# Splitting the output rows' weight pieces ahead of time, with a third place for them and loads from ACT's DMA queue

## The chip, the cores and the metric

The kernel runs on one core of a Trainium2 chip. The metric is the device time of one execution in microseconds (us), lower is better. The engines are named as in the profile: PE is TensorE's matmul, PEld its weight load, DVE is VectorE, ACT is ScalarE, POOL is GpSimd, SP is SyncE, which here only issues DMAs (SPq).

## What is computed

One layer of a streaming encoder over 2048 prompt tokens and 32 sample tokens, width 1024, all in float32. The reference, cut to what matters:

```python
h = layer_norm(x, ln_in_g, ln_in_b)
z = h @ w_in                                   # one projection for both mixers and the gates
y_a = gated_delta_net(conv4(z[qkv]), ...)      # 8 heads, blocks of 64 frames
y_b = z[B] * conv3(z[C] * z[u]) * silu(z[zb])  # short gated convolution
gates = sigmoid(z[gate])
merged = gates[:1024] * (y_a @ w_proj_a) + gates[1024:] * (y_b @ w_proj_b)
h1 = layer_norm(ALPHA * h + merged @ w_out, ln1_g, ln1_b)
ple = sigmoid(h1 @ w_ple_gate) * (p @ w_ple)
h2 = layer_norm(ALPHA * h1 + ple, ln2_g, ln2_b)
```

## The kernel before

**Precision.** Every matmul is made of three: an operand x is split into a high part `hi` (x cast to float32r) and a low part `lo = x - hi`, and the product is hi·hi + hi·lo + lo·hi. A weight piece of 128 x 1024 is split where it is first used (`load_w`): SP loads the raw piece into `wr`, ACT casts it into `wh` (L248), DVE or POOL subtracts into `wl` (L249), and SP stores both halves in DRAM (L251) for the next use, which loads the two halves (L243). `wr`, `wh` and `wl` have two places each, in the pool `wp`.

**Order of the work.** The tokens go in two halves (1024 prompt tokens and the 32 of the sample, then 1024). Each half has three parts:

1. *Projections.* A list of jobs, one for each block of 128 output columns. A job loads its weight piece, and PE makes groups of 24 matmuls of 352 (first half) or 512 columns into one of three accumulators `acc`; ACT or DVE takes the result out. `run` loads the next job's piece while a job runs. The delta rule's steps are interleaved by `fill.pump()`. The last eight jobs are gate jobs (`gate_a_job`): a sigmoid by ACT into a tile `ga`, which SP stores in DRAM.
2. *Merge* (`merge`): 24 jobs: five gate jobs for the other gate (`gb_`), eight for `w_proj_b` (`wb`), three gate jobs (`late`), eight for `w_proj_a` (`wa`), which load their gate back into `gt` (two places). `yh`, `yl` and `m` are tiles of 33,792 bytes a partition. ACT and DVE split the merged `m` into `xh`, `xl` (L970, L972).
3. *Output rows.* Here tokens are the stationary operand and weights move. `out_rows` (with `w_out`, `wo`) and then `ple_rows` (with `w_ple_gate`, `wg`) go over groups of four blocks of 128 tokens (in the first group of the first half also the sample), for each over two column halves `ch` of 512, and in each through four weight pieces `q` (`rows`). A piece serves 12 matmuls of 512 columns for each of its two k (14 with the sample's block), so 24 or 28 matmuls. When a column half is done, ACT and DVE add the residual and take statistics; when a group is done, DVE applies the LayerNorm, and PE transposes the rows (L223) into two places `pp`, from which ACT casts (L226) and DVE subtracts (L227) the next stationary operand. `pw` holds rows of p @ w_ple, which POOL multiplies with the sigmoid (L1088). `lnx` are the rows themselves. In the second half `hold` brings four pieces of `wg` into `xh`, `xl` ahead.

In the first half's rows the eight pieces of `wo` and the eight of `wg` are used for the first time, so they are split there, the subtraction by POOL. All later uses load the stored halves. All DMAs are issued by SP, in one queue.

**What sets the order.** A scheduler of the framework orders each engine's instructions at build time by priority and a model of time; on the chip each engine takes its list in order, and a tile's place is waited for by semaphore. Pools opened after others are closed lie on the same memory; their tiles wait for the tiles that lay there.

Of the kernel before, what the change touches and what calls it, by code (L numbers as in the profile page):

```python
# [20 lines left out]
NS = 32  # L21
HP = 1024
# [71 lines left out]
def hybrid_kernel(ctx: ExitStack, tc: tile.TileContext, I, O):  # L94
    nc = tc.nc
    ve, ac, po, pe = nc.vector, nc.scalar, nc.gpsimd, nc.tensor
# [3 lines left out]
    wp = ctx.enter_context(tc.tile_pool(name="wp", bufs=2))  # L100
# [59 lines left out]
    xh = cp.tile([128, KT, HP + 2 * NS], F32R, name="xh")  # L160
# [65 lines left out]
                ac.copy(out=oh, in_=p[:, :, :n])  # L226
                ve.tensor_tensor(out=lo[:, 4 * b:4 * b + 4, l0:l0 + n], in0=p[:, :, :n], in1=oh.bitcast(F32), op=ALU.subtract)  # L227

    def load_w(name, at, low, into=None):


        src, kept = I[name], split_d[name]
        for i in at:
            src, kept = src[i], kept[i]

        def cut(x):
            return x.rearrange("p (a b) -> p a b", a=2) if into else x

        parts = into or [wp.tile([128, 1024], F32R, tag=x, name=x) for x in ("wh", "wl")]
        hi, lo = parts  # L240
        if (name, at) in stored:
            for i, t in enumerate(parts):
                nc.sync.dma_start(out=t.bitcast(F32), in_=cut(kept[i]))  # L243
            return parts
        stored.add((name, at))
        raw = cut(wp.tile([128, HP + NS], F32, tag="wr", name="wr")[:, :1024])
        nc.sync.dma_start(out=raw, in_=cut(src))
        ac.copy(out=hi, in_=raw)  # L248
        low.tensor_tensor(out=lo, in0=raw, in1=hi.bitcast(F32), op=ALU.subtract)  # L249
# [643 lines left out]
    def gate_a_job(hf, c, gp):  # L893

        t = []

        def open():
            t.append(gp.tile([128, 1064], F32, tag=("ct", "cu")[c % 2], name="ga", bufs=1))

        def evac(a, g0, n):  # L900
            ac.activation(out=t[0][:, g0:g0 + n], in_=a[:, :n], func=AF.Sigmoid)

        def close():
            nc.sync.dma_start(out=ga_d[c, :, 0:hf.nt], in_=t[0][:, :hf.nt])

        return Job(("wz", BGA + c), hf.groups, evac, close, open)


    def merge(hf, mp):
        yh = mp.tile([128, KT, HP + NS], F32R, tag="yh", name="yh", bufs=1)  # L910
        m = mp.tile([128, KT, HP + NS], F32, tag="m", name="m", bufs=1)
        yl = mp.tile([128, KT, HP + NS], F32R, tag="yl", name="yl", bufs=1)

        def load_y(br, ks):
            for k in ks:
                raw = wp.tile([128, HP + NS], F32, tag="wr", name="yr")[:, :hf.nt]
                nc.sync.dma_start(out=raw, in_=y_d[br][k, :, 0:hf.nt])
                ac.copy(out=yh[:, k, :hf.nt], in_=raw)
                ve.tensor_tensor(out=yl[:, k, :hf.nt], in0=raw, in1=yh[:, k, :hf.nt].bitcast(F32), op=ALU.subtract)  # L919

        def loads_y(br, jobs):
# [12 lines left out]

        def evac_b(c, a, s):
            ve.tensor_tensor(out=m[:, c, s], in0=a[:, :s.stop - s.start], in1=m[:, c, s], op=ALU.mult)

        def evac_a(c, a, s):
            ve.tensor_tensor(out=gts[c][:, s], in0=a[:, :s.stop - s.start], in1=gts[c][:, s], op=ALU.mult)
            ve.tensor_tensor(out=m[:, c, s], in0=m[:, c, s], in1=gts[c][:, s], op=ALU.add)  # L940

        gts = {}

        def load_gate(c):
            gts[c] = mp.tile([128, HP + NS], F32, tag="gt", name="gt", bufs=2)
# [12 lines left out]
        gb_ = [gate(c, BGB, lambda c: m[:, c, :]) for c in range(5)]  # L958
        late = [late_gate(c) for c in range(5, KT)]
        wb = [branch(c, "wb", evac_b if c < 5 else plain) for c in range(KT)]  # L960
        wa = [branch(c, "wa", evac_a) for c in range(KT)]
        loads_y("b", gb_[:4])
        loads_y("a", wb[7:] + late)
        for c in range(KT):
            wa[c].open = lambda c=c: load_gate(c)
        run(gb_ + wb + late + wa)
        for g in hf.ogroups:
            for k in range(KT):
                for s in ([slice(g[0][0], g[0][0] + 512)] + ([slice(HP, HP + NS)] if len(g) > 4 else [])):
                    ac.copy(out=xh[:, k, s], in_=m[:, k, s])  # L970
                    low = xl[:, k, s] if s.start < HP else xh[:, k, HP + NS:]
                    ve.tensor_tensor(out=low, in0=m[:, k, s], in1=xh[:, k, s].bitcast(F32), op=ALU.subtract)  # L972


    def hold(q):

        load_w("wg", (1, q), po, [t[:, 2 * q:2 * q + 2, 512:HP] for t in (xh, xl)])

    def rows(src, npiece, kh, kl, cols, done, after=None, last=1):

# [12 lines left out]

        halves = [slice(0, 512), slice(512, 1024)]
        for q in range(npiece - last):
            w = load_w(*src(q), po)
            for kk in range(2):
                for a, (t0, n) in zip(accs, cols):  # L1000
                    step(a, t0, n, 2 * q + kk, *w, halves[kk])
            if after:
                after(q)
        ws = [load_w(*src(q), po) for q in range(npiece - last, npiece)]
        for a, (t0, n) in zip(accs, cols):
            for i, w in enumerate(ws):
                for kk in range(2):
# [27 lines left out]
        ve.tensor_tensor(out=t[:n], in0=t[:n], in1=a[:n], op=ALU.add)  # L1035
        return t[:n]

    def out_rows(hf, h1, lp, op, g1, b1):
        for gi, g in enumerate(hf.ogroups):
            xs, sts = [], []  # L1040
            for t0, n in g:
# [4 lines left out]
            for ch in range(2):  # L1046
                def done(a, n, i):
                    x = xs[i][:n, 512 * ch:512 * ch + 512]
                    ve.scalar_tensor_tensor(out=x, in0=x, scalar=ALPHA, in1=fold(a, n, op), op0=ALU.mult, op1=ALU.add)
                    ln_stats(sts[i], xs[i], n, ch)  # L1050

                rows(lambda q: ("wo", (ch, q)), 4, xh, xl, g, done)
            for i, (t0, n) in enumerate(g):
                ln_apply(xs[i:i + 1], n, sts[i:i + 1], g1, b1)
                nc.sync.dma_start(out=h1_d[hf.row0 + t0:hf.row0 + t0 + n, :], in_=xs[i][:n])
                fill.add(spaced(transpose_split(xs[i], n, *(h1[gi] if n > NS else h1[gi][:1] * 2), 128 * i, 128 * i + (NS if n == NS else 0)), 7 if i else 14))

    def ple_rows(hf, gi, h1, lp, op, g2, b2, end=False, hold=None, late=False):
        g = hf.ogroups[gi]
        xs, ws, sts = [], [], []  # L1060
        cols = [(128 * i, n) for i, (t0, n) in enumerate(g)]
# [14 lines left out]
        for ch in range(2):  # L1076
            pw = []
            by_tile = end and ch == 1
            for t0, n in g:
                w = op.tile([128, 512], F32, tag="pw", name="pw", bufs=4)  # L1080
                nc.sync.dma_start(out=w[:n], in_=pw_d[hf.row0 + t0:hf.row0 + t0 + n, 512 * ch:512 * ch + 512])
                pw.append(w)

# [12 lines left out]
            if by_tile:  # L1096
                rows_by_tile([(xh[:, k, 512:HP], xl[:, k, 512:HP]) for k in range(KT)], h1[gi][0], h1[gi][1], cols, done)
            else:
                rows(lambda q: ("wg", (ch, q)), 4, h1[gi][0], h1[gi][1], cols, done, (lambda q: q % 2 and hold(2 * ch + q // 2)) if hold else None, last=2 if late and ch else 1)
        if not (end or late):  # L1100
            for i in range(len(g)):
                finish(i)
# [14 lines left out]
    def ep():  # L1117
        return eps[-1]
# [17 lines left out]
    for hf in HALVES:  # L1136
        with pool(f"gp{hf.idx}") as gp:
# [28 lines left out]
            jobs += bj + [gate_a_job(hf, c, gp) for c in range(KT)]  # L1166
            fill.rate = [0.275, 0.56] if hf.sample else [0.41, 0.82]
            run(jobs, 3, *((True, lambda: deque(reload, 0)) if hf.idx else ()))
            fill.drain()
        early.close()  # L1170
        with pool(f"mp{hf.idx}") as mp:
# [3 lines left out]
        with pool(f"hp{hf.idx}") as op, pool(f"lp{hf.idx + 1}", 6) as lp, pool(f"gbp{hf.idx}") as gbp:  # L1175
# [2 lines left out]
            hs = [(h1h, h1l), (xh, xl)]  # L1178
            g1, b1, g2, b2 = gb(gbp, "ln_out", 4)
            fill.rate = [1.0, 1.0]  # L1180
            out_rows(hf, hs, lp, op, g1, b1)
            if hf.idx == 0:
                fill.add(reload_h(h1, lp, h1.blocks[4:8]))
            ple_rows(hf, 0, hs, lp, op, g2, b2, hold=hold if hf.idx else None)
            fill.drain()
            ple_rows(hf, 1, hs, lp, op, g2, b2, hf.idx == 1, late=hf.idx == 0)
            if hf.idx == 0:
                reload = reload_h(h1, lp, h1.blocks[0:4])
    for i, nm in enumerate("ps"):
# [84 lines left out]
```

## Time and profile before

| | |
|---|---|
| median of 3 runs | 3222.32 us (3219.36 to 3226.43) |
| the profiled execution's own time | 3223.0 us |
| its span, first to last instruction | 3221.3 us |
| mean granted clock of TensorE | 0.977 |
| PE busy | 3065.1 us, 95% of the span |
| DVE, ACT, POOL busy | 1911.1, 887.2, 225.4 us (59%, 28%, 7%) |
| DMA | 477.07 MB, mean 148 GB/s |
| bytes on the queue that SP issues to | 473.78 MB |

The span is what the views of the trace divide up; the time of the profiled execution is 1.7 us longer. PE is the bound of the kernel as a whole, but the share of its busy time is a mean over parts with different limits: the gate jobs of the first half run from about 1085 to 1183 us, its merge to 1462, its output rows to 1709; the second half's rows run from 2999 to 3205.

### The profile page before, as it was taken

The numbers are of one execution on the slowest core, as the hardware profiler recorded it, in microseconds if no ns is written. First come the engines' busy times: TensorE is split into PE (matmuls) and PEld (weight loads), VectorE is DVE, ScalarE is ACT, GpSimd is POOL, SyncE is SP. The second block draws the span as 40 slices with busy tenths as digits, with TensorE's granted clock in tenths as the row PEclk, the third lists the DMA queues.
The fourth block names the chain that finished last, engine by engine and source line by source line (L and its number), as shares of the span: only waits on it lengthen the run. The fifth ranks groups of instructions, "written<-read, shape, count | busy, mean of one in ns | idle before, by whom it ended". The sixth has DMA issues, their size and how long they took to land.

```text
span 3221.3 us, 51399 instructions
## 1 busy us (share of the span) xinstructions
PE 3065.1 (95%) x20524; PEld 2679.5 (83%) x20524; DVE 1911.1 (59%) x4759; ACT 887.2 (28%) x2152; POOL 225.4 (7%) x349
## 2 busy tenths in 40 slices
PE   7999999999999999999989999999999999999997
PEld 5998899999999999997767877778877788888776
DVE  6866887777877422343656568777677730123366
ACT  3333443343333221221212223333233211111010
POOL 2110000100000000002221000000000000000001
PEclk8999999999999999999989999999999999999999
DMA  7643233333333454557773322232322234444685
GB/s 281 230 151 110 91 125 115 122 121 119 117 110 121 150 199 166 181 187 256 277 259 131 119 90 84 82 96 84 96 90 85 84 110 145 158 131 133 227 299 189
DMA packets 176416, 477.07 MB, mean 148 GB/s; under 512 B 54640, under 2 KB 59280, under 8 KB 175792
## 3 DMA queue, kind: packets, MB, share of 16 engines
q1 hardware_dynamic: 176176, 473.78, 42.7%
q8 instruction: 161, 2.64, 0.3%
q14 instruction: 79, 0.65, 0.1%
HBM read 293.29 MB, written 180.41 MB: 147 GB/s over the span
## 4 chain that ended last, share of the span: by engine, by line
PE 68%; DVE 18%; issue 8%; DMA 3%; POOL 1%; ACT 1%; SPq 0%; DVEq 0%; POOLq 0%; ACTq 0%
PE acc L273 56%; DVE ktm L559 4%; DVE vtm L559 3%; DVE at L559 1%; DVE v L523 1%; PE oo L768 1%; PE sc L777 1%; PE oo L778 1%; PE sc L766 1%; POOL sg L1088 1%; PE sc L758 1%; DVE dt L609 1%; PE pp L686 1%; PE pp L629 1%; DVE lnx L206 1%
## 5 line engine op out<-in xcount | busy, mean ns | idle before, releaser
L273 PE MATMUL acc<-xh,wl 128*128 128x352 f32 (+1 forms) x3200 | 718.0, 361 | 0.0
L273 PE MATMUL acc<-xh,wh 128*128 128x352 f32 (+1 forms) x3200 | 714.5, 359 | 0.7 <-ACT xh L226 0.7
L273 PE MATMUL acc<-xl,wh 128*128 128x352 f32 (+1 forms) x3200 | 711.3, 359 | 0.0
L273 PEld LDWEIGHTS acc<-xh,wl 128*128 128x128 f32 x3200 | 553.7, 190 | 54.4 <-issue 1.6
L273 PEld LDWEIGHTS acc<-xh,wh 128*128 128x128 f32 x3200 | 552.0, 190 | 55.3 <-issue 1.4
L273 PEld LDWEIGHTS acc<-xl,wh 128*128 128x128 f32 x3200 | 551.6, 190 | 53.1 <-issue 1.8
L248 ACT CAST wh<-wr 128x1024 fp32r<-128x1024 f32 x112 | 117.3, 1048 | 266.3 <-PE acc L273 197.8
L249 DVE TENSOR_TENSOR wl<-wr,wh 128x1024 fp32r<-128x1024 f32 x96 | 117.2, 1221 | 73.6 <-PE acc L273 43.7
L919 DVE TENSOR_TENSOR yl<-yr,yh 128x1056 fp32r<-128x1056 f32 (+1 forms) x32 | 39.7, 1241 | 164.1 <-DMA ga_d<-ga 90.8
L273 PE MATMUL acc<-yh,wl 128*128 128x352 f32 (+1 forms) x640 | 133.9, 351 | 0.0
L273 PE MATMUL acc<-yl,wh 128*128 128x352 f32 (+1 forms) x640 | 133.9, 351 | 0.0
L273 PE MATMUL acc<-yh,wh 128*128 128x352 f32 (+1 forms) x640 | 133.9, 351 | 0.0
L273 PEld LDWEIGHTS acc<-yh,wh 128*128 128x128 f32 x640 | 111.5, 188 | 10.9
L273 PEld LDWEIGHTS acc<-yl,wh 128*128 128x128 f32 x640 | 111.5, 188 | 10.8
L273 PEld LDWEIGHTS acc<-yh,wl 128*128 128x128 f32 x640 | 111.5, 188 | 10.8
L559 DVE STREAM_TRANSPOSE at<-q 32x256 f32<-32x256 f32 x256 | 111.6, 436 | 11.2 <-PE pp L726 7.3
L559 DVE STREAM_TRANSPOSE ktm<-vtm 32x256 f32<-32x256 f32 x260 | 113.2, 435 | 4.0
L559 DVE STREAM_TRANSPOSE vtm<-v 32x256 f32<-32x256 f32 x256 | 111.5, 436 | 6.7 <-ACT v L524 2.5
L559 DVE STREAM_TRANSPOSE ktm<-k 32x256 f32<-32x256 f32 x256 | 111.5, 436 | 6.3 <-ACT k L524 2.2
L780 DVE SCALAR_TENSOR_TENSOR S<-S,gl,sc 128x128 f32<-128x128 f32 x136 | 46.7, 344 | 104.7 <-PE sc L777 103.2
L508 ACT COPY z<-acc 128x352 f32<-128x352 f32 (+3 forms) x144 | 61.8, 446 | 169.1 <-PE acc L273 168.8
L774 ACT ACTIVATE v<-sc,bk 128x128 f32<-128x128 f32 (+1 forms) x136 | 49.4, 363 | 207.8 <-DVE v L772 207.4
(320 smaller groups left out, 4461.3 us busy)
## 6 DMA issues: line engine op xcount, KB each, us to landing
wr<-wz SPq DMA_DIRECT2D x80, 512.0 KB, 4.4
wz_d<-wh SPq DMA_DIRECT2D x80, 512.0 KB, 2.6
wz_d<-wl SPq DMA_DIRECT2D x80, 512.0 KB, 2.9
wl<-wz_d SPq DMA_DIRECT2D x80, 512.0 KB, 4.1
wh<-wz_d SPq DMA_DIRECT2D x80, 512.0 KB, 3.4
lnx<-h_d SPq DMA_DIRECT2D x40, 512.0 KB, 5.8
h_d<-lnx SPq DMA_DIRECT2D x32, 512.0 KB, 3.1
wh<-wo_d SPq DMA_DIRECT2D x24, 512.0 KB, 4.5
```

The lines of the kernel that those rows point to most:

```text
L206: ve.scalar_tensor_tensor(out=x[:n], in0=x[:n], scalar=mv[:n, i, 0:1], in1=g[:n], op0=ALU.subtract, op1=ALU.mult)
L248: ac.copy(out=hi, in_=raw)
L249: low.tensor_tensor(out=lo, in0=raw, in1=hi.bitcast(F32), op=ALU.subtract)
L273: pe.matmul(out=a[:, :n], lhsT=wt[:, k * 128:(k + 1) * 128], rhs=xt[:, k, g0:g0 + n], start=i == 0, stop=i == 23)
L508: ac.copy(out=t["z"][:, c0:c0 + m], in_=a[:, o:o + m])
L523: ve.scalar_tensor_tensor(out=a[:, :L], in0=z[:, i:i + L], scalar=wca[:, cb, i:i + 1], in1=a[:, :L], op0=ALU.mult, op1=ALU.add)
L559: ve.transpose(out=dst[b:b + 32, :, a:a + 32], in_=src[a:a + 32, :, b:b + 32])
L609: ve.tensor_tensor_scan(out=d, data0=ones[:P, :P], data1=d, initial=0.0, op0=ALU.mult, op1=ALU.add)
L629: pe.matmul(out=p[:, c, :], lhsT=k[:, 4 * b + c, :], rhs=k[:, 4 * b + c, :], start=True, stop=True)
L774: ac.activation(out=v1, in_=pt, func=AF.Copy, scale=bk[:, col])
L780: ve.scalar_tensor_tensor(out=Sc, in0=Sc, scalar=sc["gl"][:, col], in1=pd, op0=ALU.mult, op1=ALU.add)
L919: ve.tensor_tensor(out=yl[:, k, :hf.nt], in0=raw, in1=yh[:, k, :hf.nt].bitcast(F32), op=ALU.subtract)
```

## The change

1. The 16 pieces `wo` and `wg` are split earlier, by a new function `split`: the eight of `wo` one at the opening of each of the first half's last eight gate jobs, the eight of `wg` at the opening of one `gb_` job and seven `wb` jobs of the first half's merge. The raw piece goes into a place of `wr`, ACT casts, DVE (before: POOL) subtracts, into two places of `z` (gate jobs) or of `gt` (merge) that are free there. The two stores are issued at the next split (`store_left`).
2. In the rows all pieces are loaded as stored halves, and ACT issues these loads (`queue=ac`); `hold`'s loads stay on SP.
3. Every third load of a piece in the rows goes to a third place, two tiles with the tag `za`, in the pool `ep1` in the first half and in the rows' own pool `op` in the second.
4. `pw` has eight places in place of four in the second half. `store_split` and `later` come in, but nothing is put into `later`.

```diff
-    def load_w(name, at, low, into=None):
+    def load_w(name, at, low, into=None, halves=False, extra=None, queue=nc.sync):
...
+        store_split()
+        if extra is not None:
+            turn[0] += 1
+            if turn[0] % 3 == 0:
+                into = [extra().bitcast(F32R) for _ in "hl"]
...
         if (name, at) in stored:
             for i, t in enumerate(parts):
-                nc.sync.dma_start(out=t.bitcast(F32), in_=cut(kept[i]))
+                queue.dma_start(out=t.bitcast(F32), in_=cut(kept[i]))
             return parts
...
             t.append(gp.tile([128, 1064], F32, tag=("ct", "cu")[c % 2], name="ga", bufs=1))
+            if hf.idx == 0:
+                split(*pieces[c], lambda: ep().tile([128, 1064], F32, tag="z", name="gs", bufs=2))
...
+    def split(name, at, buf):
+        raw = wp.tile([128, HP + NS], F32, tag="wr", name="sr")[:, :1024]
+        nc.sync.dma_start(out=raw, in_=I[name][at[0]][at[1]])
+        store_left()
+        hi, lo = [buf()[:, :1024].bitcast(F32R) for _ in "hl"]
+        ac.copy(out=hi, in_=raw)
+        ve.tensor_tensor(out=lo, in0=raw, in1=hi.bitcast(F32), op=ALU.subtract)
+        stored.add((name, at))
+        left.extend((t, split_d[name][at[0]][at[1]][i]) for i, t in enumerate((hi, lo)))
+
+    def store_left():
+        while left:
+            t, d = left.pop(0)
+            nc.sync.dma_start(out=d, in_=t.bitcast(F32))
+
+    pieces = [(n, (ch, q)) for n in ("wo", "wg") for ch in range(2) for q in range(4)]
...
+        if hf.idx == 0:
+            def buf():
+                return mp.tile([128, HP + NS], F32, tag="gt", name="gs", bufs=2)
+
+            for i, j in enumerate(gb_[4:] + wb[:7]):
+                j.open = lambda p=pieces[8 + i]: split(*p, buf)
+            wb[7].open = store_left
...
-            w = load_w(*src(q), po)
+            w = load_w(*src(q), po, extra=third, queue=ac)
...
-        ws = [load_w(*src(q), po) for q in range(npiece - last, npiece)]
+        ws = [load_w(*src(q), po, extra=third, queue=ac) for q in range(npiece - last, npiece)]
...
-                w = op.tile([128, 512], F32, tag="pw", name="pw", bufs=4)
+                w = op.tile([128, 512], F32, tag="pw", name="pw", bufs=8 if hf.idx else 4)
...
             run(jobs, 3, *((True, lambda: deque(reload, 0)) if hf.idx else ()))
+            store_left()
             fill.drain()
...
-            out_rows(hf, hs, lp, op, g1, b1)
+
+            def third(p=op if hf.idx else ep()):
+                return p.tile([128, HP + NS], F32, tag="za", name="xw", bufs=2)[:, :1024]
+
+            out_rows(hf, third, hs, lp, op, g1, b1)
```

## Rows read from the trace of the kernel before

**Rows 1.** Busy time of the engines by stretch: the first half's gate jobs, its merge, its output rows, and the second half's output rows. Columns: stretch and its length in us, busy us of PE, PEld, DVE, ACT and POOL (with instructions), mean granted clock of TensorE, busy share of the DMA engines, GB/s.

```profile
1085.00:1183.00 98.00, 98.00 (x575) 86.39 (x575) 22.90 (x58) 25.14 (x59) 0.00 (x0) 1.00 0.43 153
1183.00:1462.00 279.00, 279.00 (x1728) 279.00 (x1727) 100.56 (x140) 62.58 (x87) 2.40 (x1) 1.00 0.53 185
1462.20:1709.10 246.90, 218.98 (x943) 168.32 (x942) 123.33 (x327) 42.71 (x66) 60.62 (x34) 0.94 0.73 261
2997.30:3205.20 207.90, 193.57 (x841) 154.50 (x840) 105.97 (x300) 18.98 (x32) 17.90 (x12) 0.97 0.72 258
```

**Rows 2.** Waits of PE in the first half's output rows (1462 to 1710 us), by what ended them: us in total, times, longest us.

```profile
PE sc L989 <- DMA wl<-wg_d: 6.7, 2, 4.1
PE sc L988 <- DMA wh<-wg_d: 5.3, 2, 4.9
PE sc L988 <- ACT wh L248: 4.8, 2, 2.8
PE oo L988 <- ACT wh L248: 3.6, 1, 3.6
PE sc L989 <- POOL wl L249: 2.2, 2, 1.2
PE acc L988 <- DMA wh<-wg_d: 1.3, 1, 1.3
PE oo L989 <- POOL wl L249: 1.2, 1, 1.2
...
PE sc L989 <- DMA wl<-wo_d: 0.6, 1, 0.6
```

**Rows 3.** The same view of the second half's output rows (2997 to 3206 us).

```profile
PE oo L988 <- DMA wh<-wo_d: 5.5, 1, 5.5
PE pp L223 <- DVE xl L227: 3.9, 1, 3.9
PE sc L989 <- DMA wl<-wg_d: 2.1, 2, 1.3
PE oo L989 <- DMA wl<-wg_d: 1.3, 1, 1.3
PE acc L989 <- DMA wl<-wo_d: 0.9, 1, 0.9
PE oo L988 <- DMA wh<-wg_d: 0.6, 1, 0.6
```

**Rows 4.** PE in order of time around 1481 us: start, us of one or of a merged run, line, output and inputs, count; in brackets the idle time before it and what ended it.

```profile
1481.55 0.40 PE L989 MATMUL sc<-wl,xh 128*64 128x512 f32 x1
1485.56 0.80 PE L988 MATMUL oo<-wh,xh 128*128 128x512 f32 x1 [3.61 <-ACT wh L248]
...
1488.00 0.79 PE L989 MATMUL oo<-wl,xh 128*128 128x512 f32 x1 [1.22 <-POOL wl L249]
1488.59 0.63 PE L991 MATMUL oo<-wh,xl 128*128 128x512 f32 x1
...
1494.13 0.39 PE L989 MATMUL acc<-wl,xh 128*128 128x512 f32 x1
```

**Rows 5.** The same view around 1671 us.

```profile
1671.07 1.22 PE L988 MATMUL sc<-wh,xh 128*128 128x512 f32 x2 [4.92 <-DMA wh<-wg_d]
...
1677.20 0.79 PE L989 MATMUL sc<-wl,xh 128*128 128x512 f32 x1 [4.06 <-DMA wl<-wg_d]
...
1681.97 0.39 PE L991 MATMUL oo<-wh,xl 128*128 128x512 f32 x1
```

**Rows 6.** SP's queue in order of time around 1668 us: start, us (with its wait, where several are merged), line, transfer, count.

```profile
1665.36 0.73 SPq L243 DMA_DIRECT2D wh<-wg_d  x1
1668.15 2.25 SPq L1072 DMA_DIRECT2D out_y<-lnx  x2
...
1670.91 0.44 SPq L243 DMA_DIRECT2D wl<-wg_d  x1
```

**Rows 7.** DMA issues of the whole span by transfer: count, KB each, median us from issue to landing.

```profile
wh<-wo_d SPq DMA_DIRECT2D x24, 512.0 KB, 4.5
...
wr<-wo SPq DMA_DIRECT2D x8, 512.0 KB, 5.8
```

**Rows 8.** Busy time by stretches of 20 us, columns as in rows 1: the stretch with the most bytes among those read.

```profile
3000.00:3020.00 20.00, 14.54 (x56) 11.27 (x55) 1.47 (x3) 0.62 (x1) 0.00 (x0) 0.83 0.99 389
```

**Rows 9.** Groups of instructions by cost, of the whole span: line, engine, operation, output and inputs, count, busy us, mean ns of one, idle time before them and what ended most of it.

```profile
L248 ACT CAST wh<-wr 128x1024 fp32r<-128x1024 f32 x112 | 117.3, 1048 | 266.3 <-PE acc L273 197.8
L249 DVE TENSOR_TENSOR wl<-wr,wh 128x1024 fp32r<-128x1024 f32 x96 | 117.2, 1221 | 73.6 <-PE acc L273 43.7
```

**Rows 10.** The start of the second half's output rows in order of time: first SP's queue, then DVE's last read of `m` before it.

```profile
3002.22 1.76 SPq L1043 DMA_DIRECT2D lnx<-h_d  x4
3004.98 0.32 SPq L243 DMA_DIRECT2D wh<-wo_d  x1
...
3001.50 0.69 DVE L972 TENSOR_TENSOR xl<-m,xh 128x512 fp32r<-128x512 f32 x1 [0.69 <-ACT xh L970]
```

**Rows 11.** PE in the same stretch: the first matmul of the rows, the last of the second piece (the 48th), and the first of the third piece.

```profile
2999.19 0.40 PE L988 MATMUL oo<-wh,xh 128*128 128x512 f32 x1
...
3010.15 0.40 PE L991 MATMUL acc<-wh,xl 128*128 128x512 f32 x1
3016.01 0.77 PE L988 MATMUL oo<-wh,xh 128*128 128x512 f32 x1 [5.46 <-DMA wh<-wo_d]
```

More of the change, by code (lines that the diff above doesn't have):

```diff
@@ L227, in transpose_split, with store_split @@
                 ve.tensor_tensor(out=lo[:, 4 * b:4 * b + 4, l0:l0 + n], in0=p[:, :, :n], in1=oh.bitcast(F32), op=ALU.subtract)
-    def load_w(name, at, low, into=None):
+    turn = [0]
+    later = []
+    def store_split():
+        while later:
+            t, d = later.pop(0)
+            nc.sync.dma_start(out=d, in_=t.bitcast(F32))
+    def load_w(name, at, low, into=None, halves=False, extra=None, queue=nc.sync):
         src, kept = I[name], split_d[name]
@@ L234, in load_w @@
             src, kept = src[i], kept[i]
+        store_split()
[3 more added lines that the diff above has]
+                into = [extra().bitcast(F32R) for _ in "hl"]
         def cut(x):
-            return x.rearrange("p (a b) -> p a b", a=2) if into else x
+            return x.rearrange("p (a b) -> p a b", a=2) if halves else x
         parts = into or [wp.tile([128, 1024], F32R, tag=x, name=x) for x in ("wh", "wl")]
@@ L975, in hold, with rows @@
     def hold(q):
-        load_w("wg", (1, q), po, [t[:, 2 * q:2 * q + 2, 512:HP] for t in (xh, xl)])
-    def rows(src, npiece, kh, kl, cols, done, after=None, last=1):
+        load_w("wg", (1, q), po, [t[:, 2 * q:2 * q + 2, 512:HP] for t in (xh, xl)], True)
+    def rows(third, src, npiece, kh, kl, cols, done, after=None, last=1):
         accs = [wide_acc() for _ in cols]
@@ L1036, in fold, with out_rows @@
         return t[:n]
-    def out_rows(hf, h1, lp, op, g1, b1):
+    def out_rows(hf, third, h1, lp, op, g1, b1):
         for gi, g in enumerate(hf.ogroups):
@@ L1050, in done @@
                     ln_stats(sts[i], xs[i], n, ch)
-                rows(lambda q: ("wo", (ch, q)), 4, xh, xl, g, done)
+                rows(third, lambda q: ("wo", (ch, q)), 4, xh, xl, g, done)
             for i, (t0, n) in enumerate(g):
@@ L1056, in out_rows, with ple_rows @@
                 fill.add(spaced(transpose_split(xs[i], n, *(h1[gi] if n > NS else h1[gi][:1] * 2), 128 * i, 128 * i + (NS if n == NS else 0)), 7 if i else 14))
-    def ple_rows(hf, gi, h1, lp, op, g2, b2, end=False, hold=None, late=False):
+    def ple_rows(hf, third, gi, h1, lp, op, g2, b2, end=False, hold=None, late=False):
         g = hf.ogroups[gi]
@@ L1098, in ple_rows @@
             else:
-                rows(lambda q: ("wg", (ch, q)), 4, h1[gi][0], h1[gi][1], cols, done, (lambda q: q % 2 and hold(2 * ch + q // 2)) if hold else None, last=2 if late and ch else 1)
+                rows(third, lambda q: ("wg", (ch, q)), 4, h1[gi][0], h1[gi][1], cols, done, (lambda q: q % 2 and hold(2 * ch + q // 2)) if hold else None, last=2 if late and ch else 1)
         if not (end or late):
@@ L1180, in hybrid_kernel @@
             fill.rate = [1.0, 1.0]
-            out_rows(hf, hs, lp, op, g1, b1)
+            def third(p=op if hf.idx else ep()):
+                return p.tile([128, HP + NS], F32, tag="za", name="xw", bufs=2)[:, :1024]
+            out_rows(hf, third, hs, lp, op, g1, b1)
             if hf.idx == 0:
                 fill.add(reload_h(h1, lp, h1.blocks[4:8]))
-            ple_rows(hf, 0, hs, lp, op, g2, b2, hold=hold if hf.idx else None)
+            ple_rows(hf, third, 0, hs, lp, op, g2, b2, hold=hold if hf.idx else None)
             fill.drain()
-            ple_rows(hf, 1, hs, lp, op, g2, b2, hf.idx == 1, late=hf.idx == 0)
+            ple_rows(hf, third, 1, hs, lp, op, g2, b2, hf.idx == 1, late=hf.idx == 0)
             if hf.idx == 0:
```

2 lines of the change are left out of this document (added).

## The prediction, made before the changed kernel ran

> **What bounds the kernel now.** I read the busy time of the engines by stretch first, because the edits touch four stretches and no others. In the stretch of the first half's gate jobs and in its merge PE is busy the whole time, at full clock; in the output rows of the two halves it is not: 27.9 us of 246.9 idle and a mean granted clock of 0.94 in the first half, 14.3 of 207.9 and 0.97 in the second [rows 1]. The reader is to see that the time to win lies in the rows alone, and that whatever is added to gate jobs and merge runs beside a PE that must not be stopped.
>
> Next, who PE waits for. In the first half's rows eight of the entries are weight pieces: 13.9 us for DMAs that bring stored halves (6.7, 5.3, 1.3, 0.6), 8.4 for ACT's cast of a new piece (4.8, 3.6), 3.4 for POOL's subtraction (2.2, 1.2): 25.7 us together [rows 2]. In the second half's rows pieces cost 5.5 us once at the start and 2.1 + 1.3 + 0.9 + 0.6 = 4.9 after it; 3.9 us there is DVE's share of a transposition, no weight [rows 3].
>
> Then PE's own timeline, for the price of a wait beyond the wait. After the stall at 1481.55 the matmuls take 0.63 us in place of 0.39 until 1494.13 [rows 4], after that at 1665 until 1681.97 [rows 5]; those are the two levels of the clock, 1.2 and 2.4 GHz, and half of the busy time at the lower one is lost: (8.6 - 1.2) / 2 = 3.7 us and (10.9 - 4.1) / 2 = 3.4 us. A third such stretch follows the 2.8 us wait for a cast; I estimate it at 2.5 from these two.
>
> Last, SP's queue, for why a stored piece is late. Around 1665 loads of pieces stand between stores of finished rows, which wait for DVE: the second load of the late piece is issued only at 1670.91, after two stores that began at 1668.15 and took 2.25 us [rows 6]. The transfer itself has a median of 4.5 us [rows 7], less than the 24 matmuls of a piece (48 take 10.96 + 0.23 us from 2999.19 on [rows 11], so 24 take 5.6). So order in one queue is late, more than bytes.
>
> **The change part by part.**
>
> *Splits leave the rows.* Sixteen pieces no longer pass raw load, cast and subtraction there: ACT's 8.4 us and POOL's 3.4 us go with the causes, and two of the slow stretches, 3.7 + 2.5. Gain 18.0.
>
> *Loads leave SP's queue, with three places in place of two.* A load is issued when the piece three before it is done, two pieces or 11 us ahead of need, against a landing of 4.5 to 5.8 us (the median of a raw load of these weights) [rows 7], and no store of finished rows stands before it. So the 13.9 us of DMA waits and the 3.4 of slow clock go in the first half: 17.3. In the second half 4.9 goes. On ACT the issues cost little: about 120 of some 0.4 us (SP's own issues) [rows 6] over 455 us in which ACT is busy 62 [rows 1]. SP keeps the rows' own loads and stores and `hold`'s pieces, now without pieces in front; nothing of PE's waits for those is in the lists, so no gain is taken. The eight `pw` places only free SP.
>
> Bytes: in the first half's rows 261 GB/s over 246.9 us is 64.4 MB; 16 x 1.57 MB go (raw load, two stores), 16 x 1.05 come, 56 MB in some 212 us, 264 GB/s. The trace has a stretch with 389 GB/s at a busy share of 0.99 [rows 8]. So the rate fits on the average.
>
> The Trainium skill (DMA: Bandwidth & Descriptors, Issuing engines are not separate DMA queues) says that DMAs of all issuers run on the same 16 engines and that a second issuer saves only issue time. The trace of before has no piece on a second queue, so it cannot say; if the rule's "only" held here, the second rival below would be the result.
>
> *Sixteen splits arrive elsewhere.* Per block one cast of 1.05 us on ACT, one subtraction of 1.22 on DVE [rows 9], one raw load and two stores. ACT is at 26% and 22% of the two stretches, DVE at 23% and 36% [rows 1]; a job lasts 279 / 24 = 11.6 us. Bytes: 8 x 1.57 MB over some 95 us add 132 GB/s to 153 and 185, at most 317, again under 389. The raw places (two) are shared with the jobs' own raw loads, which then have one place each; such a load still has a whole job, 11.6 us, for a landing of about 6. What hides all this is three accumulators: a group lasts 3.9 us, so an evacuation may come 7.8 us late before PE notices. I cost it at nothing; bounds 0 and, if a hold goes past that slack, the last rival.
>
> *The second half's first piece.* This speaks against the change. The third place is used at every third load; the first half has 32, so the second half's first piece, the 33rd, goes to the place in `op`. There it comes after `h1h` and `h1l`, 18,432 + 16,384 bytes a partition, on memory that the merge held: `yh` has 33,792, so the place lies on `m`. That memory of `m` is waited for whole is shown by the rows' first `lnx` loads, issued at 3002.22, just when the last read of `m` ends (3001.50 + 0.69) [rows 10]. Now the first rows matmul starts at 2999.19 with its piece long there [rows 11]; changed, the load is issued at about 3002.3. Landing: 4.5 us by the median [rows 7], or 11.0 by the piece that was issued at 3004.98 behind the same burst and used at 3016.01 [rows 10, 11]. PE then stands 7.5 to 14.0 us, plus 3.5 at the lower clock as after the other long stalls: 11.0 to 17.5, I take 14.0, since the burst of `lnx` and `ln_out` is there again. In its place goes today's stall for the third piece, 5.5 and 2.0 at the lower clock. Net loss 6.5 (3.5 to 10.0).
>
> The Trainium skill (same page, Queues, rings and completion order) says that each DMA engine takes turns between queues by packets. By that the piece would get half of 389 GB/s behind SP's burst, an estimate of 5.4 us of transfer, and the sum would be nearer the lower bound; no run here shows it yet.
>
> *New waits.* Faster PE means that pieces two and three of the first half's rows, issued when the merge ends, land among the same burst of row loads. Bounds 0 and one stall like that of [rows 4], 3.6 + 1.2 + 3.7 = 8.5; I take 3, because the first of them has 6.5 us and the second 13 (a piece of the first group is 28 matmuls).
>
> Sum: -18.0 - 17.3 - 4.9 + 6.5 + 3.0 = -30.7. The profiled execution took 3223.0 (its span is 3221.3), 0.7 over the median shown; so 3222.3 - 30.7 = 3191.6.
>
> **Rivals.** *The place in `op` costs nothing or more is hidden:* 30.7 + 14.0 + 3.0 = 47.7 less, 3175. For it: only that the order of the pool is read from the code; against it the `lnx` loads.
>
> *The DMA engines are late, not SP's queue:* the DMA waits and their slow stretch stay (17.3 and 4.9) and only the splits' 18.0 goes; -18.0 + 6.5 + 3.0 = -8.5, 3214. For it: busy shares of 0.73 and 0.72 over whole stretches [rows 1]; against it [rows 6].
>
> *ACT becomes the queue that is late.* A load that waits on ACT for PE to leave a place holds what is queued behind it: casts of transposed rows (13 tiles in the first half, 8 in the second, two casts each, 42) and the sigmoids. PE waits for such a cast through two `pp` tiles. From 0.7 us of such waiting a cast (30.7 / 42) the gain is gone: 3222. Against it: while the load waits, PE still has two pieces, and PE's transpositions stand in the same order.
>
> *Slower:* in gate jobs and merge the split's cast stands on ACT ahead of an evacuation and waits for its raw load or for the place that the stores of the block before must leave. If ACT is held past 7.8 us, PE stops in each of 16 blocks; 1.9 us a block (30.7 / 16) cancels the gain, 3 us give 3191.6 + 48 = 3240. For it: two raw places for twice the loads, and three times the stores and loads in one queue. Against it: PE waits for nothing there now, and ACT has three quarters of its time free [rows 1].
>
> **How the numbers follow.** Forecast 0.58 (its own range 3186 to 3201: both lower bounds, both upper ones); more gain 0.08; DMA engines 0.16; ACT's queue 0.09; slower 0.09. Faster by over 0.2% (6.4 us, about what a measurement of this kernel can tell from no change): 0.58 + 0.08 + 0.15 = 0.81; within 0.2%: 0.08; slower: 0.11, the last rival and a fifth of the ACT case. The range 3175 to 3215 holds the first three cases.
>
> **What would show it.** Right: no wait of PE for an ACT cast or POOL subtraction in the first half's rows, the clock there at 0.98 or more, that stretch about 32 us shorter; PE still without a wait in gate jobs and merge; a wait of PE of 8 to 14 us for a DMA at the start of the second half's rows, for a piece in the third place. Wrong: waits for `wh` or the third place by DMA all through the rows (DMA engines), PE waiting for `pp` behind ACT, or any PE wait between 1060 and 1460.

## The result, and the profile after

The changed kernel takes 3184.7 us (median of 4 runs, 3180.3 to 3187.3) against 3224.4 for the kernel before in the same series: 39.7 us less, a ratio of 0.9879 with a 95% interval of 0.9863 to 0.9895. A later series gave 0.9881 (0.9864 to 0.9897). So it is faster by 33 to 44 us; 30.7 were forecast.

The profiled execution of the changed kernel has a span of 3178.6 us. Its lines are 15 to 44 higher: L258 are the stored loads, L288 the jobs' matmuls, L1032 to L1035 those of the rows, L1131 the sigmoid. The busy time of the engines in the stretches of [rows 1], gate jobs, merge, and the two halves' rows:

```profile
1085.00:1183.00 98.00, 98.00 (x575) 86.39 (x575) 30.41 (x63) 30.77 (x67) 0.00 (x0) 1.00 0.72 255
1183.00:1460.50 277.50, 277.50 (x1719) 277.50 (x1718) 107.07 (x147) 68.59 (x92) 0.00 (x0) 1.00 0.63 224
1460.50:1681.00 220.50, 208.51 (x938) 164.00 (x937) 123.34 (x339) 28.22 (x51) 25.81 (x19) 0.98 0.74 261
2960.90:3165.70 204.80, 190.41 (x841) 153.97 (x839) 111.35 (x313) 18.79 (x33) 18.56 (x12) 0.96 0.74 264
```

In gate jobs and merge PE is busy for every microsecond, as before, although ACT, DVE and the DMA engines do the sixteen splits there (DMA share 0.72 and 0.63). The first half's rows are 26.4 us shorter and run at 0.98 of the clock, not 0.94. The second half's are only 3 us shorter: PE is idle there for 14.4 us, as before (14.3).

PE's waits in the first half's rows, all of them, which answer to [rows 2]:

```profile
PE acc L1032 <- DMA wh<-wg_d: 8.2, 2, 6.8
PE pp L223 <- DVE xl L227: 2.0, 2, 1.7
PE oo L1033 <- DMA xw<-wo_d: 1.8, 1, 1.8
```

No ACT cast and no POOL subtraction is left. In the second half's rows [rows 3] two are left, both for the third place `xw`:

```profile
PE oo L1032 <- DMA xw<-wo_d: 13.5, 1, 13.5
PE oo L1033 <- DMA xw<-wo_d: 0.9, 1, 0.9
```

The 13.5 us are the wait that was foretold, at the place that was foretold. ACT's and SP's timelines at the merge's end, and PE's:

```profile
2965.73 21.37 ACTq L258 DMA_DIRECT2D xw<-wo_d  x4
```

```profile
2964.40 0.33 SPq L1150 DMA_DIRECT2D ln_out<-ln_out  x1
2965.73 13.39 SPq L1087 DMA_DIRECT2D lnx<-h_d  x6
```

```profile
2976.34 0.77 PE L1032 MATMUL oo<-xw,xh 128*128 128x512 f32 x1 [13.47 <-DMA xw<-wo_d]
2976.90 0.63 PE L1032 MATMUL acc<-xw,xh 128*128 128x512 f32 x1
```

The load of `xw` goes out at 2965.73, in the same moment as the first `lnx` load on the other queue: both waited for the last read of `m`. PE's first matmul with it comes 10.6 us later, and PE goes on at 0.63 us a matmul.

The tail is 3 us shorter: the last matmul starts 13.3 us before the span's end, not 16.3. Here are ACT and DVE at the tail, first of the kernel before, then of the changed one:

```profile
3205.39 0.60 ACT L1087 ACTIVATE sg<-acc 128x512 f32<-128x512 f32 x1 [4.94 <-PE acc L1021]
```

```profile
3206.87 1.27 DVE L206 SCALAR_TENSOR_TENSOR lnx<-lnx,ln_mv,ln_out 128x1024 f32<-128x1024 f32 x1
...
3208.63 1.28 DVE L209 SCALAR_TENSOR_TENSOR lnx<-lnx,nw_y,ln_out 128x1024 f32<-128x1024 f32 x1
3209.91 0.68 DVE L1088 TENSOR_TENSOR sg<-pw,sg 128x512 f32<-128x512 f32 x1
```

```profile
3165.69 0.60 ACT L1131 ACTIVATE sg<-acc 128x512 f32<-128x512 f32 x1 [4.94 <-PE acc L1065]
```

```profile
3165.32 1.28 DVE L209 SCALAR_TENSOR_TENSOR lnx<-lnx,nw_y,ln_out 128x1024 f32<-128x1024 f32 x1
...
3167.16 0.69 DVE L1132 TENSOR_TENSOR sg<-pw,sg 128x512 f32<-128x512 f32 x1
```

Before, the last sigmoid ended at 3205.99, and DVE's product with it started 3.92 us later, behind L206 and L209 of an earlier row tile. After, it starts 0.87 us later, with one L209 in front. DVE's order in each trace is that of its list in the built program, and the lists differ: before, L206 and a second L209 stand between that first L209 and the last product; after, only the small operations of a LayerNorm.

### The profile page after: what moved, and what is told of

It is laid out like the page before. It is cut to its first block, busy times and chain, and to the rows that moved or that the text cites. A ratio compares the mean times of both kernels' runs of the same rounds, so it can differ in the third digit from the quotient of the medians.

```text
span 3178.6 us, 51454 instructions
## 1 busy us (share of the span) xinstructions
PE 3048.5 (96%) x20524; PEld 2673.7 (84%) x20524; DVE 1926.2 (61%) x4775; ACT 886.1 (28%) x2152; POOL 187.5 (6%) x333
## 4 chain that ended last, share of the span: by engine, by line
PE 73%; DVE 18%; issue 5%; DMA 2%; ACT 1%; POOL 0%; SPq 0%; DVEq 0%; ACTq 0%; POOLq 0%
PE acc L288 57%; DVE ktm L574 4%; DVE vtm L574 3%; DVE v L538 1%; DVE at L574 1%; PE acc L1035 1%; PE acc L1033 1%; PE acc L1032 1%; PE oo L783 1%; PE sc L792 1%; PE sc L781 1%; PE oo L793 1%; PE sc L773 1%; PE pp L701 1%; DVE dt L624 1%
## 5 line engine op out<-in xcount | busy, mean ns | idle before, releaser
L288 PE MATMUL acc<-xh,wl 128*128 128x352 f32 (+1 forms) x3200 | 716.7, 360 | 0.0
L288 PE MATMUL acc<-xl,wh 128*128 128x352 f32 (+1 forms) x3200 | 713.5, 360 | 0.0
L288 PE MATMUL acc<-xh,wh 128*128 128x352 f32 (+1 forms) x3200 | 710.8, 358 | 0.0
L288 PEld LDWEIGHTS acc<-xh,wl 128*128 128x128 f32 x3200 | 553.3, 190 | 54.3 <-issue 1.6
L288 PEld LDWEIGHTS acc<-xl,wh 128*128 128x128 f32 x3200 | 552.7, 190 | 53.4 <-issue 1.8
L288 PEld LDWEIGHTS acc<-xh,wh 128*128 128x128 f32 x3200 | 549.4, 189 | 53.7 <-issue 1.4
L263 ACT CAST wh<-wr 128x1024 fp32r<-128x1024 f32 x96 | 100.6, 1048 | 147.5 <-PE acc L288 137.2
L956 DVE TENSOR_TENSOR yl<-yr,yh 128x1056 fp32r<-128x1056 f32 (+1 forms) x32 | 39.7, 1241 | 158.8 <-DMA ga_d<-ga 90.6
L288 PE MATMUL acc<-yl,wh 128*128 128x352 f32 (+1 forms) x640 | 133.9, 351 | 0.0
L288 PE MATMUL acc<-yh,wh 128*128 128x352 f32 (+1 forms) x640 | 133.9, 351 | 0.0
L288 PE MATMUL acc<-yh,wl 128*128 128x352 f32 (+1 forms) x640 | 133.9, 351 | 0.0
L288 PEld LDWEIGHTS acc<-yh,wh 128*128 128x128 f32 x640 | 111.5, 188 | 10.9
L288 PEld LDWEIGHTS acc<-yh,wl 128*128 128x128 f32 x640 | 111.5, 188 | 10.8
L288 PEld LDWEIGHTS acc<-yl,wh 128*128 128x128 f32 x640 | 111.5, 188 | 10.8
```

Source lines behind the costliest of these rows:

```text
L288: pe.matmul(out=a[:, :n], lhsT=wt[:, k * 128:(k + 1) * 128], rhs=xt[:, k, g0:g0 + n], start=i == 0, stop=i == 23)
```

## The experiments

Ten more runs were made, two of them with an unaltered kernel. The later series have the kernel before at 3222.0, 3220.2 and 3217.5 us. For each trace I cut the span at PE's first matmul of the rows, the first job of the second half, the last job group of the second half's merge, and the end. The two kernels with two traces tell how much of a difference is spread. A trace is of one execution, which need not lie at the median of its kernel: that of "no third place" took 3217.2 us, that of "SP's queue" 3202.9, that of "third later" 3182.2.

| kernel | median, us | ratio (95%) | first rows matmul to the next half's first job | to that half's last job group | from there to the end |
|---|---|---|---|---|---|
| before, two traces | 3224.4, 3215.0 (one execution) | | 251.2, 250.8 | 1283.9, 1279.9 | 224.0, 221.4 |
| changed, two traces | 3184.7, 3181.4 | 0.9879, 0.9881 | 224.2, 223.3 | 1276.1, 1282.6 | 217.7, 217.0 |
| splits only | 3207.8 | 0.9962 (0.9950 to 0.9974) | 241.9 | 1284.0 | 218.8 |
| no third place | 3207.1 | 0.9958 (0.9942 to 0.9973) | 239.8 | 1285.3 | 228.8 |
| SP's queue | 3197.1 | 0.9924 (0.9909 to 0.9939) | 236.4 | 1285.0 | 218.2 |
| third later | 3174.6 | 0.9851 (0.9837 to 0.9866) | 229.0 | 1279.3 | 206.3 |
| `pw` four | 3184.8 | 0.9894 (0.9876 to 0.9913) | 224.5 | 1276.5 | 216.8 |
| third in `wr` | 3166.0 | 0.9834 (0.9815 to 0.9852) | 227.6 | 1274.6 | 199.7 |
| four places | 3159.7 | 0.9807 (0.9789 to 0.9826) | 225.0 | 1278.7 | 200.7 |
| last piece alone | 3184.4 | 0.9891 (0.9872 to 0.9911) | 219.8 | 1281.8 | 217.0 |

### What each part is worth: three kernels with one part undone

```diff
-            w = load_w(*src(q), po, extra=third, queue=ac)
+            w = load_w(*src(q), po, queue=nc.sync)        # splits only
+            w = load_w(*src(q), po, queue=ac)             # no third place
+            w = load_w(*src(q), po, extra=third, queue=nc.sync)   # SP's queue
```

(the same in the line of the last pieces)

> The splits are moved as in the changed kernel; the rows load their stored halves from SP's queue again, into two places. The theory (order in SP's queue makes stored pieces late, the splits cost 18.0 of their own) expects the 18.0 of the splits to be gone and PE's DMA waits for pieces to stay at some 14 us in the first half's rows and 10 in the second's, no 13.5 us wait at the start of the second half's rows: about 3224 - 18 = 3206, and a few less if the shorter ends of groups and tail come with this part. The rival (the stores and raw loads in SP's queue were the delay; with them gone the queue is free) expects PE's DMA waits to be mostly gone too: about 3180, below the changed kernel, since the wait at the second half's start is not there.

> The changed kernel without the third place: pieces in two places, issued by ACT. A load then goes out one piece, 5.6 us, ahead of need, and the landing medians of ACT's queue are 4.5 to 5.4. The theory that the queue is the cure expects hardly a wait in the rows and no 13.5 us wait at the start of the second half's rows: 3170 to 3178, below the changed kernel. The theory that the third place's lead is needed expects many waits of 0.5 to 2 us in both halves' rows, with PE at the lower clock after some: 3190 or more.

> The changed kernel with the pieces' loads on SP's queue again, three places kept. If the order in SP's queue (pieces behind stores of finished rows that wait for DVE) makes pieces late, waits of PE for pieces of 1 to 7 us at the ends of groups stay: 3190 to 3200. If the lead of the third place is enough by itself, or the DMA engines set the landing, it is within 4 us of the changed kernel, 3181 to 3188. The wait of 13.5 us at the second half's start is there in both.

Splits only: 3207.8, near the theory's number. PE's waits in that trace, first half's rows (its longest two), then the second's (two):

```profile
PE sc L1032 <- DMA wh<-wg_d: 10.9, 2, 8.9
PE oo L1032 <- DMA wh<-wo_d: 4.7, 1, 4.7
...
PE oo L1032 <- DMA wh<-wo_d: 5.6, 1, 5.6
PE sc L1033 <- DMA wl<-wg_d: 2.6, 2, 1.5
```

The casts are gone and the DMA waits stay: with three smaller ones, 18.4 us in the first half's rows, more than the 13.9 of [rows 2]. The longest, 8.9 us, stands before the same matmul of the rows (the 713th) as the first of the two waits of [rows 5], 4.9 + 4.1 us for the same piece: it did not change. The 4.7 us for `wo`, which end at 1481.79, are new: they stand before the 57th matmul, the third piece, whereas the waits for cast and subtraction, 3.6 + 1.2 [rows 2, 4], stood at the fourth.

No third place: 3207.1, not to be told from splits only by intervals that are some 5 us wide either way. So of ACT's queue by itself no gain shows. Its waits are many and short, nine entries in the first half's rows (one of them DVE's) and seven in the second's, of which the longest are:

```profile
PE acc L1032 <- DMA wh<-wg_d: 6.0, 2, 4.2
PE oo L1033 <- DMA wl<-wo_d: 3.6, 2, 2.1
...
PE oo L1032 <- DMA wh<-wo_d: 4.2, 3, 1.8
PE acc L1032 <- DMA wh<-wo_d: 3.6, 1, 3.6
```

That is the second theory of that run, the lead: with two places a load goes out one piece, 5.6 us, ahead, and landings of 4.5 to 5.8 us [rows 7] leave nothing over.

SP's queue: 3197.1, 10.7 less than splits only, 12 to 16 more than the changed kernel. The time is the one expected for a late queue, the waits are not: the short ones are mostly gone, and one of 14.4 us stands in the first half's rows beside the one at the second half's start:

```profile
PE acc L1032 <- DMA wh<-wg_d: 14.4, 1, 14.4
PE oo L1032 <- DMA xw<-wo_d: 4.3, 1, 4.3
...
PE oo L1032 <- DMA xw<-wo_d: 16.4, 1, 16.4
```

SP's queue before the end of those 14.4 us, at 1668.23:

```profile
1657.11 2.25 SPq L1116 DMA_DIRECT2D out_y<-lnx  x2
...
1659.92 2.05 SPq L1125 DMA_DIRECT2D pw<-pw_d  x4
1662.06 0.38 SPq L258 DMA_DIRECT2D wh<-wg_d  x1
```

PE ran dry at 1653.8; the piece's load is issued at 1662.06, behind two stores of finished rows and the loads of `pw`. That is the order in SP's queue that the prediction spoke of. So the gain of 23 us beyond the splits needs both: neither the lead nor the queue has it alone.

### Where the third place lies

```diff
+            turn[0] = 0                                   # third later
             out_rows(hf, third, hs, lp, op, g1, b1)
...
             def third(p=op if hf.idx else ep()):
+                if hf.idx:                                # third in wr
+                    return wp.tile([128, HP + NS], F32, tag="wr", name="xw")[:, :1024]
```

> The changed kernel, but the count of pieces starts anew in the second half, so that its first two pieces go to the old places and the third piece to the third place, 11 us later than now. The theory (the first piece waits for the memory that m held until 2965.7, then 10.6 us for its landing) expects the 13.5 us wait to shrink to some 4 us (landing at about 2976, needed at 2961 + 11 = 2972) and part of the slow clock with it: 9 to 13 less than the changed kernel, 3171 to 3176. The rival (the burst of rows and gains makes whatever piece comes first late) expects a wait of 8 us or more for the first or second piece and no more than 4 us gained.

> The changed kernel, but in the second half the third place is the two places of wr, which nobody uses in the rows and which are free well before the merge ends. The theory (the first piece waits for the memory of m, then for its landing behind the burst) expects the 13.5 us wait and the clock loss behind it to be gone: 15 to 18 less than the changed kernel, 3167 to 3170, and some 5 less than the run that only moved the third place to the third piece. The rival (the burst of row loads makes the first pieces late wherever they lie) expects no more than that run: 3174 or more.

Third later: 3174.6, 7 to 10 us less than the changed kernel, the theory's case. In its second half's rows these are all of PE's waits, 3.7 us where some 4 were expected:

```profile
PE oo L1033 <- DMA xw<-wo_d: 2.0, 1, 2.0
PE oo L1032 <- DMA xw<-wo_d: 1.7, 1, 1.7
```

Third in `wr`: 3166.0, 18.8 less than the same series' kernel with four `pw` places, which equals the changed one. From the last job group to the last matmul:

```profile
2963.00:3149.80 186.80, 186.80 (x841) 151.84 (x840) 111.28 (x313) 18.80 (x32) 18.60 (x12) 1.00 0.78 284
```

PE is busy for all 186.8 us at full clock, with no wait. The gain is a little more than the 15 to 18 that were expected. The burst of row loads is the same, and a piece issued beside it at 2963.24 lands as late as in the changed kernel (KB, and us from issue to landing):

```profile
wh<-wo_d ACTq DMA_DIRECT2D x1, 512.0 KB, 10.4
wl<-wo_d ACTq DMA_DIRECT2D x1, 512.0 KB, 11.1
```

But that is the third piece, which PE needs some 11 us after the first; the first lies in memory that is long idle and is there when the rows begin. So the wait was the memory of `m`, and with it the slow landing that a load issued so late meets. Its price is made of the changed kernel's own row above: 204.8 - 190.4 = 14.4 us idle, and 190.4 - 186.8 = 3.6 us of slow clock, 18.0 together.

### The places of `pw`

```diff
-                w = op.tile([128, 512], F32, tag="pw", name="pw", bufs=8 if hf.idx else 4)
+                w = op.tile([128, 512], F32, tag="pw", name="pw", bufs=4)
```

> The changed kernel with four places for pw in the second half, as before. The theory that the eight places are what took DVE's transposition wait (3.9 us) out of the second half's rows and shortened the tail behind the last matmul (16.1 to 13.1 us) expects both back: 4 to 8 slower than the changed kernel, 3189 to 3193. The rival (they only free SP, as the prediction had it; tail and transposition wait follow from the pieces coming on time) expects no difference: 3182 to 3188, tail 13 us.

3184.8: no difference that the intervals could tell, and they could not tell the smaller of the 4 to 8 us that my guess after the result expected. The trace decides: the tail is 13.3 us with four places too, and PE has no transposition wait in the second half's rows. So `pw` explains neither; nothing speaks against the prediction's "only free SP". The tail is 16.3 us in both traces of the kernel before, 16.9 in splits only, and 13.3 in every trace that has the third place or ACT's queue. DVE's last operations stand in one order in both traces of before, in another in splits only, and in a third in all the others. What in the build tips that order stays open, and so does which of them took away the transposition wait of 3.9 us [rows 3], which the second trace of before has again and splits only has not.

### The last piece of the first half's rows

Of the waits left in the first half's rows the longest, 6.8 us, is for the last piece of all. ACT's queue and SP's in the changed kernel:

```profile
1653.22 0.33 ACTq L258 DMA_DIRECT2D wh<-wg_d  x1
1660.79 0.33 ACTq L258 DMA_DIRECT2D wl<-wg_d  x1
1661.41 0.33 ACTq L258 DMA_DIRECT2D wh<-wg_d  x1
```

```profile
1652.82 1.78 SPq L1116 DMA_DIRECT2D out_y<-lnx  x2
1654.65 3.57 SPq L1125 DMA_DIRECT2D pw<-pw_d  x4
1660.34 0.80 SPq L348 DMA_DIRECT2D lnx<-h_d  x2
```

PE had left the last piece's place by about 1653.5, and ACT had nothing else to do; still the load went out at 1660.79. The built program names what it waits for. In it each DMA gets one of eight completion counts in turn, across both queues, and a DMA that gets a count waits for the one that had it before:

```
ACT L258 load wl (last piece)   waits: PE; the load three pieces before it; store out_y, SP L1116 (same count)
ACT L258 load wh (last piece)   waits: PE; load pw, SP L1125 (same count)
SP  L348 load lnx (second)      waits: load wl of the piece before; the same store out_y
```

The store is the second `out_y` of the row above. Its issue, and the time from issue to landing:

```profile
1654.26 0.34 SPq L1116 DMA_DIRECT2D out_y<-lnx  x1
out_y<-lnx SPq DMA_DIRECT2D x1, 128.0 KB, 6.5
```

So it lands at 1660.7, and `wl` goes out at 1660.79. SP's second `lnx` load, which waits for the same store, goes out in the same moment (1660.34 and 0.80 for the two). Issued at 1653.5 the piece would have had 8.8 us until PE ran dry at 1662.3; from `wl`'s issue at 1660.79 to the end of PE's wait at 1669.1 it took 8.3. So the count explains the whole wait, by this estimate. In the trace of "third later", the same program in this half, the same events follow one another:

```profile
1661.45 0.33 ACTq L258 DMA_DIRECT2D wh<-wg_d  x1
1670.55 0.34 ACTq L258 DMA_DIRECT2D wl<-wg_d  x1
```

```profile
1662.64 1.09 SPq L1116 DMA_DIRECT2D out_y<-lnx  x2
...
1670.19 0.80 SPq L348 DMA_DIRECT2D lnx<-h_d  x2
```

Stores, last piece and row load are all 9.8 us later than in the changed kernel. 8.2 of these are a shift of the whole trace (the piece two before the last is issued at 1650.47, not 1642.31); the load keeps to the store, and PE waits 10.4 us. So a load on ACT's queue is still held by SP's stores, and those by DVE. Two kernels take that piece on.

```diff
             turn[0] += 1
-            if turn[0] % 3 == 0:
+            if turn[0] % 4 == 0:                          # four places
                 into = [extra().bitcast(F32R) for _ in "hl"]
+            elif turn[0] % 4 == 3:
+                into = [wp.tile([128, HP + NS], F32, tag="wr", name="xr")[:, :1024].bitcast(F32R) for _ in "hl"]
...
-                rows(third, ..., last=2 if late and ch else 1)
+                rows(third, ..., last=1)                  # last piece alone
```

> Four places in both halves: after the two old ones the two of wr for every third, the third place for every fourth piece. In the second half the place in op is then first needed for the fourth piece, 17 us after the rows begin. In the first half the last piece of the rows goes out one piece earlier, and in the built program it no longer waits for the completion count of a store of finished rows. The theory (the 6.8 to 10.4 us wait of PE for that piece is the coupling of ACT's loads to SP's stores, and the second half's start is the memory of m) expects both waits to be gone: 23 to 27 less than the changed kernel, 3157 to 3162. If the wait for the last piece is the DMA engines' own, it stays and the run is near 3168.

> The changed kernel without the pairing of the last two pieces in the first half's last column half. PE then needs the last piece 5.6 us later, while it is issued as before. The theory that this piece is issued late (it waits for a store of finished rows) expects PE's wait for it to shrink from 7 to 10 us to 2 to 4, and, if the four row tiles that now finish closer together cost nothing, 4 to 8 less: 3177 to 3181. The rival (the time is taken back, because the rows' last DVE work then ends later against the next half's first jobs) expects no gain: 3183 to 3187.

Four places: 3159.7, in the expected band, the best of all here and 25 us under the changed kernel, most of it by the second half's start. No wait for the last piece is left. In PE's waits of the first half's rows and the transition, DVE stands in its place:

```profile
PE pp L223 <- DVE xl L227: 7.6, 3, 4.2
PE oo L1035 <- DMA wl<-wo_d: 2.2, 1, 2.2
```

What its going is worth isn't shown: the median is 6.3 us under third in `wr`, with overlapping intervals, and the first half's stretch of 225.0 us lies among the 223.3 to 229.0 of the five traces whose program is the same there (the changed kernel's two, third later, `pw` four, third in `wr`). So most of that wait is given back, or all. Whether the missing store in its list of waits or the earlier issue freed the piece, this kernel doesn't tell apart.

Last piece alone: the wait shrinks to 3.8 us, and the time is 3184.4, the rival's number; a gain of some 4 us would not show in intervals of 6 us either way. The busy times of the 60 us after the rows, and PE's waits in them, of the changed kernel and of this one:

```profile
1682.90:1742.90 60.00, 57.30 (x263) 43.74 (x262) 43.44 (x131) 22.12 (x44) 5.69 (x13) 1.00 0.42 137
PE pp L223 <- DVE xl L227: 2.6, 3, 1.0
```

```profile
1677.40:1737.40 60.00, 55.18 (x246) 41.94 (x245) 44.92 (x135) 20.98 (x42) 6.65 (x12) 0.94 0.36 122
PE pp L223 <- DVE xl L227: 4.8, 3, 3.6
```

PE leaves the rows earlier, but DVE, which still has the rows' LayerNorms and the next half's transpositions to do, has not come as far: PE waits 4.8 us for it in place of 2.6, at a clock of 0.94. So behind the late piece DVE is the next to be waited for.

### The spread of the unaltered kernels

> The changed kernel once more, unaltered, for a second trace. What lies between the two halves' rows was 8.5 us shorter in its first trace than in that of the kernel before, though its code is the same. If that is the change's (DVE and the queues stand otherwise when the next half begins), the stretch is again 1276 to 1279 us; if it is the spread between executions, it lies anywhere from 1276 to 1285. PE's wait for the last piece of the first half's rows should be 6 to 11 us, and the one at the second half's start 12.5 to 14.5.

> The kernel before once more, unaltered, for a second trace: the stretch between the two halves' rows 1281 to 1287 us if its length belongs to the kernel, and 16 us from the last matmul to the end if the tail's length belongs to the order in which DVE's instructions stand.

The stretch between the halves' rows was 8 us shorter in the first trace of the changed kernel than in that of before; the second traces have it 3 us longer. It is spread, not the change's; the second trace of before has 1279.9, a little under the 1281 to 1287 that were expected if the length belonged to the kernel. The rows are not spread: 224.2 and 223.3 against 251.2 and 250.8, and the second half's rows with the tail 217.7 and 217.0 against 224.0 and 221.4.

## Why the prediction was right, and where not

The sign is right, and the time of 3184.7 lies in the range of 3175 to 3215; it is 1.3 us under the forecast's own range, 3186 to 3201, whose lower end stands for 36.7 less, while 39.7 and 36.1 were measured in the two series. By stretches: for the first half's rows -32.3 was forecast (-18.0 - 17.3 + 3.0), measured -27.0 and -27.5; for the second half +1.6, measured -4 to -6. The two errors go against each other: that the stretches together, 32 to 33 us less, come so near the 30.7 is luck. The 4 to 6 us more that the medians have are placed by no trace.

- **Splits cost nothing where they arrive: right.** No PE wait between 1060 and 1459 in any of the traces; the slower rival has no place left.
- **Splits leave the rows, 18.0: mechanism right, size off.** Alone they took 14.1 off the median, and 9 in the first half's rows. PE's waits for cast and subtraction went, but its DMA waits there rose from 13.9 to 18.4 us, by the new 4.7 for `wo`.
- **Loads leave SP's queue with three places, 17.3 + 4.9: right as a pair, sized too small.** With the loss at the second half's start and the new waits the sum had 12.7 for the pair (17.3 + 4.9 - 6.5 - 3.0); the medians have 23. I had credited the queue order with most of it; the runs show no gain of that order without the lead, and 10.7 us of the lead without the order. What I did not see is that a load on ACT's queue stays tied to SP's DMAs by the completion counts, and with it a wait of 6 to 10 us for the last piece. This is not the third rival, in which a load holds ACT's casts: here the load itself is held, and ACT had nothing else to do.
- **The second half's first piece, 14.0 less today's 7.5: place and mechanism right, size too small.** The landing was 10.6 us, near my upper bound of 11.0, PE stood 13.5 + 0.9, and taking the cause away gave 18.8. The term that was too small is the stall, which I took near the middle of its bounds; the slow clock, 3.5 in the sum, was 3.6.
- **New waits, 3.0: right in the kind** (1.8 us, once, for the third place).
- **The DMA engines as the limit: wrong.** With the share at 0.78 PE has no wait at all. The rule of the Trainium skill (DMA: Bandwidth & Descriptors, Issuing engines are not separate DMA queues) that a second issuer saves only issue time agrees with the run without the third place (3207.1 against 3207.8), and not with the 12 to 16 us that ACT's queue is worth beside the third place: there the order of issue counts, as SP's queue at 1662.06 shows. The rule of the Trainium skill on turns by packets (same page, Queues, rings and completion order) I had turned into half of the rate and 5.4 us; the trace has nearly as many packets on either queue, 272 and 302, but not as many bytes (last section), and the piece took 10.6.
- **Not in the sum at all:** 3 us of tail, by the order of DVE's instructions, and 3.9 us of a transposition wait, whose going is not explained; and the clock of the second half's small waits, which were taken without one. Against the 186.8 us that these matmuls take at full clock, PE was busy 193.6 before and 190.4 after: 3.2 us less at the lower clock, where the sum had 2.0 less and 3.5 more.

## What to carry to other kernels

Moving loads to a second queue showed no gain here without a place more to issue them early, and the place alone had less than half of what the two have together; try the two together, and price each alone. A new buffer in a pool that lies on memory still being read is paid at its first use: look for a tile that is idle by then, as `wr` was here (18.8 us). A second queue need not be independent: look in the built program for what its DMAs wait for. Before shortening a wait, ask who is second: the last piece's wait hid DVE's lateness, and with part of it gone the time did not measurably move.

## What was not expected of the hardware

A piece of two 512 KB loads issued beside a burst of row loads on the other queue reached PE after 10.6 us, against a median of 4.5 to 5.8 for one load [rows 7]. The two queues of the changed kernel in the 10 us from 2966.2, SP's (q1) and ACT's (q10, which the kernel before does not have):

```profile
q1 hardware_dynamic: 302, 2.67, 72.2%
q10 hardware_dynamic: 272, 1.00, 25.2%
```

The packets are nearly even, the bytes (in MB) are not: a packet of SP's burst is 2.4 times as large on the average, so ACT's queue moved 27% of the bytes. The piece's 1.05 MB at that pace, 100 GB/s, are 10.5 us, an estimate that fits the 10.6. In third in `wr`, where the rows ran with a DMA share of 0.78 and 284 GB/s without one wait of PE, loads beside the burst landed no sooner (10.4 and 11.1 us); they were only issued earlier than they were needed. So the mean share said little about a single landing, and the lead hid it.
